# Low parts of every fourth stationary weight piece formed by a negated copy and an accumulating DMA

## Chip, cores and metric

The kernel runs on one core of a Trainium2 chip. The metric is the device time of one execution in microseconds (us). Times of instructions are taken from the hardware profile of one execution.

## What is computed

A trunk of two residual layers on 256 positions of width 2048, all in float32. Layer 0 is sparse attention (an indexer scores all causal keys, each query keeps 64 keys, grouped-query softmax attention follows), layer 1 a gated short convolution; a squared-ReLU MLP of width 8192 stands behind each. Cut to what matters here:

```python
def reference(x, positions, ...):
    for i in range(DEPTH):                       # DEPTH = 2
        j = i // N_MIXERS
        if i % N_MIXERS == 0:
            x = x + _dsa_mixer(_rmsnorm(x, attn_norm_g[j]), attn_w_in[j], ..., attn_w_out[j], positions)
        else:
            x = x + _short_conv_mixer(_rmsnorm(x, conv_norm_g[j]), conv_w_in[j], conv_w[j], conv_w_out[j])
        x = x + _sqrelu_mlp(_rmsnorm(x, mlp_norm_g[i]), mlp_w1[i], mlp_w2[i])
    return x

def _sqrelu_mlp(h, w1, w2):
    a = jax.nn.relu(h @ w1)
    return (a * a) @ w2
```

Nearly all the work is the product of 256 rows with 391 MB of weights, each weight being used once.

## The kernel before

**High and low parts.** A float32 product is made of three products of a shorter format (float32r): each operand is split into a high part (the value rounded) and a low part (the value less its high part), and high x high, high x low and low x high are added in PSUM.

**Pieces.** The weights are cut into 736 pieces, in the order of use. A piece is two k-tiles of 128 rows by 512 columns, laid out as 128 x 1024 elements (in the first two input projections and at the very end one k-tile of 1024 or 1104 columns). Pieces belong to units: one unit accumulates one block of output in PSUM over 4, 8 or 16 pieces, and its end function then takes the banks away. The first 64 pieces (input projection of the attention) and the last 16 have the weights as the moving operand. The 656 between them are "tall": the weights are stationary, and for each 128 x 128 block two matmuls run, line 233 with the high part against 512 columns (high and low parts of the activations) and line 234 with the low part against 256 columns (`matmuls`, lines 219 to 241). A piece is eight such pairs. All tall units begin at a piece number that is a multiple of 4.

**Loads.** One load brings two pieces (1 MB) into one of four `raw` buffers (`load_raw`, lines 178 to 189), issued by SyncE's queue, in order. `split(p)` (lines 196 to 217) makes the two parts of piece p: ScalarE copies the raw piece into `wh`, in float32r (line 211), and VectorE subtracts, `wl` = raw - wh (line 212). Behind the second piece of a load its raw buffer is given up, and the load four ahead of it is issued into the same buffer (line 217).

**Order.** The order on every engine is that in which the program is written: the main loop issues the matmuls of piece p, then the unit's end function if p is its last piece, then one step of every live generator (`step_all`), then the splits up to piece p + 4. `wh` and `wl` have five buffers each, so the split of piece p + 4 can begin when TensorE is through with piece p - 1. Generators are the follow-up work of units that have ended. Of them these matter here: `h_gen` behind each unit of w1 (folds the two halves of each bank on ScalarE and VectorE, lines 825 and 826, squares on VectorE, line 850, then multiplies twice by the row factors on GpSimd, line 856, and `put_pair` writes the `hq` tiles, lines 818 and 819); `y_gen` and `by_gen` of the convolution (GpSimd multiplications in lines 895 and 919); and `rowsT_gen`, which at each norm runs three rounds of a square-root iteration on GpSimd (`newton`, lines 255 to 258, then line 376). Before the change GpSimd issues no DMA.

Of the kernel before, what the change touches and what calls it, by code (L numbers as in the profile page):

```python
# [11 lines left out]
F32 = mybir.dt.float32  # L12
F32R = mybir.dt.float32r
I32 = mybir.dt.int32
AF = mybir.ActivationFunctionType
ALU = mybir.AluOpType
# [57 lines left out]
def trunk(ctx: ExitStack, tc: tile.TileContext, x, positions, attn_norm_g, attn_w_in, attn_q_norm_g,  # L74
          attn_k_norm_g, attn_w_out, conv_norm_g, conv_w_in, conv_w, conv_w_out, mlp_norm_g,
          mlp_w1, mlp_w2, inv, out):
    nc = tc.nc
# [10 lines left out]
    def sbt(shape, tag, bufs, dt=F32):  # L88
        return sb.tile(shape, dt, name=nm(tag), tag=tag, bufs=bufs)

    def shift(n):

        sb.tile([P, n // 4], F32, name=nm("shift"))
# [97 lines left out]
    def load(r):  # L191
        if r < len(raws):
            for _ in load_raw(r):
                pass

    def split(p):
        if p >= len(pieces):
            return
        u, i, r = pieces[p]
        w = u.kk * u.n  # L200
        src = raw_tiles[r][:, (i % 2) * w : (i % 2 + 1) * w]
        if p == 0:
            shift(448)
        hi = sbt([P, WPITCH], "wh", AHEAD + 1, F32R)
        if p == 0:
            shift(64)
        lo = sbt([P, WPITCH], "wl", AHEAD + 1, F32R)
        c = 0
        for v in u.widths if p == 0 else [w]:
            a = slice(c, c + v)  # L210
            nc.scalar.activation(hi[:, a], src[:, a], AF.Copy)  # L211
            nc.vector.tensor_tensor(lo[:, a], src[:, a], hi[:, a].bitcast(F32), ALU.subtract)  # L212
            c += v
        piece_tiles[p] = (hi, lo)
        if p + 1 == len(pieces) or pieces[p + 1][2] != r:
            del raw_tiles[r]
            load(r + RAWS)
# [821 lines left out]
    ps = None  # L1039
    step_all()  # L1040
    split(0)
    split(1)
    live.append(const_gen())
    live.append(rope_tables())
    ahead = 2
    for p in range(len(pieces)):
        matmuls(p)
        u, i, _ = pieces[p]
        if i == u.ticks - 1:
            u.end(u.banks)  # L1050
            u.banks = None
            if u.then is not None:
                live.append(u.then())
        step_all()
        while ahead < p + 1 + (AHEAD if p >= 6 else 2):
            split(ahead)
            ahead += 1
        if p == 15:
            TP = 3
# [22 lines left out]
```

## Time and profile before

| | |
|---|---|
| time, median of 2 runs | 2078.76 us (2078.75 to 2078.77) |
| time of the profiled execution | 2079.38 us |
| its span in the profile | 2077.6 us |
| mean granted clock of TensorE | 1.0 of full speed |
| busy: TensorE / VectorE / ScalarE / GpSimd | 2071.3 / 1446.3 / 1056.9 / 298.8 us |
| loads of weights | 390.94 MB on SyncE's queue |

The span is the time from the first to the last instruction in the profile; the execution's own time is somewhat longer. A busy share is an average over the span. What an engine's idle time is worth depends on whether anything on the chain that ended last waits for that engine. Engines are named as in the profile: PE is TensorE's matmul, PEld its weight load, DVE is VectorE, ACT ScalarE, POOL GpSimd, SP SyncE; an engine's name with a q is its instruction queue. A row of a timeline has the start, the duration, the engine, the line, the operation and its operands, and in brackets how long the engine was idle before it and what released it.

### The profile page before, as it was taken

To read this page: it belongs to the slowest core of one execution; us is meant where nothing else is said; L and a number is where in the kernel's file an instruction comes from. 1 tells how busy PE (TensorE), PEld (TensorE's weight loads), DVE (VectorE), ACT (ScalarE), POOL (GpSimd) and SP (SyncE) were. 2 spreads that over 40 slices of the span, in tenths; PEclk is the share of its full clock that TensorE was granted. 3 is DMA by queue.
4 is the path that set the end of the run, shared out by engine and by line. 5 is a ranking of instruction groups with operands and counts; after the bars stand their busy time and mean duration, and the time that the engine had idled before them with its cause. 6 is when DMAs were issued, how large, how long until landed. Compare 5 with 4: busy or idle time off the path is not lost.

```text
span 2077.6 us, 29879 instructions
## 1 busy us (share of the span) xinstructions
PE 2071.3 (100%) x11880; PEld 1818.1 (88%) x11880; DVE 1446.3 (70%) x1841; ACT 1056.9 (51%) x1549; POOL 298.8 (14%) x294
## 2 busy tenths in 40 slices
PE   9999999999999999999999999999999999999999
PEld 9878888888888888888888888888888888888887
DVE  6487777767667676767866676667676776767755
ACT  7456555544445444544644454555454544545443
POOL 1233105100101001010231110132010010100100
PEclk9999999999999999999999999999999999999999
DMA  8544356566565665665556655565656656665563
GB/s 300 162 142 163 132 177 199 186 200 196 189 203 183 199 191 197 195 193 196 190 182 203 200 185 185 200 188 199 191 193 203 187 196 186 202 199 186 189 193 106
DMA packets 191836, 392.86 MB, mean 189 GB/s; under 512 B 6752, under 2 KB 8016, under 8 KB 191696
## 3 DMA queue, kind: packets, MB, share of 16 engines
q1 hardware_dynamic: 191664, 390.94, 58.6%
q8 instruction: 93, 1.52, 0.3%
q14 instruction: 47, 0.39, 0.1%
q10 hardware_dynamic: 32, 0.01, 0.0%
HBM read 388.83 MB, written 2.10 MB: 188 GB/s over the span
## 4 chain that ended last, share of the span: by engine, by line
PE 99%; DMA 0%; SPq 0%; DVE 0%; issue 0%; DVEq 0%
PE ps L233 57%; PE ps L234 29%; PE ps L240 4%; PE ps L239 4%; PE ps L238 3%; PE ps L723 1%; PE ps L569 0%; PE ps L781 0%; DMA hq<-in_x 0%; PE ps L768 0%; PE ps L431 0%; PE ps L708 0%; SPq L998 0%; PE ps L301 0%; PE ps L364 0%; DVE hq L449 0%
## 5 line engine op out<-in xcount | busy, mean ns | idle before, releaser
L212 DVE TENSOR_TENSOR wl<-raw,wh 128x1024 fp32r<-128x1024 f32 (+2 forms) x738 | 945.6, 1284 | 394.1 <-ACT wh L211 391.0
L211 ACT ACTIVATE wh<-raw 128x1024 fp32r<-128x1024 f32 (+2 forms) x738 | 779.2, 1058 | 517.8 <-PE ps L233 438.0
L233 PE MATMUL ps<-xp,wh 128*128 128x512 f32 x2816 | 960.1, 389 | 0.0
L233 PE MATMUL ps<-hq,wh 128*128 128x512 f32 x2432 | 829.3, 390 | 0.0
L234 PE MATMUL ps<-xp,wl 128*128 128x256 f32 x2816 | 777.3, 276 | 0.0
L234 PE MATMUL ps<-hq,wl 128*128 128x256 f32 x2432 | 671.3, 276 | 0.0
L233 PEld LDWEIGHTS ps<-xp,wh 128*128 128x128 f32 x2816 | 528.6, 188 | 109.4
L233 PEld LDWEIGHTS ps<-hq,wh 128*128 128x128 f32 x2432 | 456.5, 188 | 95.1 <-issue 0.5
L234 PEld LDWEIGHTS ps<-xp,wl 128*128 128x128 f32 x2816 | 528.6, 188 | 0.1
L234 PEld LDWEIGHTS ps<-hq,wl 128*128 128x128 f32 x2432 | 456.5, 188 | 0.5 <-issue 0.5
L825 ACT ACTIVATE half<-ps 128x256 f32<-128x256 f32 x464 | 164.1, 382 | 280.2 <-PE ps L234 280.0
L826 DVE TENSOR_TENSOR tmp<-ps,half 128x256 f32<-128x256 f32 x464 | 183.6, 419 | 172.1 <-ACT half L825 171.9
L856 POOL TENSOR_TENSOR tmp<-tmp,tmp 128x512 f32<-128x512 f32 x64 | 123.8, 1953 | 1086.3 <-DVE tmp L850 594.7
L238 PE MATMUL ps<-wh,xp 128*128 128x512 f32 (+2 forms) x288 | 113.4, 394 | 0.0
L240 PE MATMUL ps<-wl,xp 128*128 128x512 f32 (+2 forms) x288 | 108.0, 375 | 0.3 <-DVE wl L212 0.3
L239 PE MATMUL ps<-wh,xp 128*128 128x512 f32 (+2 forms) x288 | 107.9, 375 | 0.0
L415 DVE TENSOR_TENSOR xT<-xT,tmp 128x512 f32<-128x512 f32 x144 | 99.3, 731 | 0.0
L818 ACT ACTIVATE hq<-tmp 128x512 fp32r<-128x512 f32 x72 | 45.5, 632 | 96.8 <-POOL tmp L856 73.2
L819 DVE TENSOR_TENSOR hq<-tmp,hq 128x512 fp32r<-128x512 f32 x72 | 82.1, 1141 | 5.6 <-ACT hq L818 5.6
L353 POOL TENSOR_TENSOR tmp<-tmp,tmp 128x512 f32<-128x512 f32 x21 | 38.6, 1836 | 254.5 <-ACT tmp L352 185.0
L239 PEld LDWEIGHTS ps<-wh,xp 128*128 128x128 f32 x288 | 54.2, 188 | 10.5 <-issue 2.4
L238 PEld LDWEIGHTS ps<-wh,xp 128*128 128x128 f32 x288 | 54.2, 188 | 10.2 <-issue 2.4
(139 smaller groups left out, 741.1 us busy)
## 6 DMA issues: line engine op xcount, KB each, us to landing
raw<-in_mlp_w SPq DMA_DIRECT2D x256, 1024.0 KB, 5.3
raw<-in_conv_w_in SPq DMA_DIRECT2D x48, 1024.0 KB, 5.2
raw<-in_attn_w_in SPq DMA_DIRECT2D x24, 1024.0 KB, 5.4
raw<-in_attn_w_out SPq DMA_DIRECT2D x16, 1024.0 KB, 5.1
raw<-in_conv_w_out SPq DMA_DIRECT2D x16, 1024.0 KB, 5.1
raw<-in_attn_w_in SPq DMA_DIRECT2D x4, 1104.0 KB, 9.4
raw<-in_attn_w_in SPq DMA_DIRECT2D x7, 552.0 KB, 8.5
out_y<-hq SPq DMA_DIRECT2D x7, 256.0 KB, 2.9
```

Of the source, the lines that this page charges most:

```text
L211: nc.scalar.activation(hi[:, a], src[:, a], AF.Copy)
L212: nc.vector.tensor_tensor(lo[:, a], src[:, a], hi[:, a].bitcast(F32), ALU.subtract)
L233: nc.tensor.matmul(o, wh, xk, start=(k == 0), stop=False)
L234: nc.tensor.matmul(o[:, 0:256], wl, xk[:, 0:256], start=False, stop=(k == K - 1))
L238: nc.tensor.matmul(o[:, :w], ah, wh, start=(k == 0), stop=False)
L239: nc.tensor.matmul(o[:, :w], al, wh, start=False, stop=False)
L240: nc.tensor.matmul(o[:, :w], ah, wl, start=False, stop=(k == K - 1))
L415: nc.vector.tensor_tensor(v, v, r[i], ALU.add)
L819: nc.vector.tensor_tensor(lo, val, hi.bitcast(F32), ALU.subtract)
L825: nc.scalar.activation(h, ps[:, 256:512], AF.Copy)
L826: nc.vector.tensor_tensor(dst, ps[:, 0:256], h, ALU.add)
L856: nc.gpsimd.tensor_tensor(r3, r3, rows_of(key[:-1], "rs2"), ALU.mult)
```

## The change

In tall units, for pieces whose number is 1 mod 4 (the second piece of every second load, 164 pieces), VectorE's subtraction is replaced. ScalarE writes the negated high part into `wl` (line 213 of the new program), and GpSimd issues a DMA that adds the raw piece to it in place (line 214). The other pieces are made as before.

```diff
         for v in u.widths if p == 0 else [w]:
             a = slice(c, c + v)
             nc.scalar.activation(hi[:, a], src[:, a], AF.Copy)
-            nc.vector.tensor_tensor(lo[:, a], src[:, a], hi[:, a].bitcast(F32), ALU.subtract)
+            if u.tall and p % 4 == 1:
+                nc.scalar.activation(lo[:, a], hi[:, a].bitcast(F32), AF.Copy, scale=-1.0)
+                nc.gpsimd.dma_start(lo[:, a], src[:, a], accum_op=ALU.add)
+            else:
+                nc.vector.tensor_tensor(lo[:, a], src[:, a], hi[:, a].bitcast(F32), ALU.subtract)
             c += v
```

Line numbers behind the edit are four higher in the new program: 856 becomes 860, 376 becomes 380, 255 to 258 become 259 to 262.

On GpSimd, at the end of the first MLP's square-root iteration, the program before has this order (the numbers in names are counters of the build):

```order
L258 TENSOR_TENSOR tmp_3404<-tmp_3404,tmp_3402 128x256
L376 TENSOR_TENSOR tmp_3404<-tmp_3404 128x256
L856 TENSOR_TENSOR tmp_3420<-tmp_3420,tmp_3404 128x512
L856 TENSOR_TENSOR tmp_3453<-tmp_3453,tmp_3404 128x512
L856 TENSOR_TENSOR tmp_3613<-tmp_3613,tmp_3404 128x512
L856 TENSOR_TENSOR tmp_3648<-tmp_3648,tmp_3404 128x512
```

At the same place on GpSimd the changed program has the accumulating DMAs among them:

```order
L262 TENSOR_TENSOR tmp_3415<-tmp_3415,tmp_3413 128x256
L380 TENSOR_TENSOR tmp_3415<-tmp_3415 128x256
L214 DMA wl_3494<-raw_3269 128x1024
L214 DMA wl_3579<-raw_3372 128x1024
L860 TENSOR_TENSOR tmp_3431<-tmp_3431,tmp_3415 128x512
L860 TENSOR_TENSOR tmp_3464<-tmp_3464,tmp_3415 128x512
L860 TENSOR_TENSOR tmp_3626<-tmp_3626,tmp_3415 128x512
L860 TENSOR_TENSOR tmp_3661<-tmp_3661,tmp_3415 128x512
L214 DMA wl_3693<-raw_3498 128x1024
L214 DMA wl_3783<-raw_3583 128x1024
```

An accumulate now stands directly behind the iteration, and one directly behind the multiplications of line 860; GpSimd takes its instructions in order.

On SyncE's queue the order is unchanged, and the waits differ. Four loads in the middle of the program, before:

```order
L187 DMA raw_7851<-in_mlp_w 128x4x512 [waits DMAHW2_49,DVE_49]
L187 DMA raw_7908<-in_mlp_w 128x4x512 [waits DMAHW3_49,DVE_49]
L187 DMA raw_7962<-in_mlp_w 128x4x512 [waits DMAHW4_49,DVE_49]
L187 DMA raw_8017<-in_mlp_w 128x4x512 [waits DMAHW5_49,DVE_49]
```

The same four loads on SyncE's queue now (DMASW names a semaphore of GpSimd's DMAs, DMAHW one of SyncE's):

```order
L187 DMA raw_7906<-in_mlp_w 128x4x512 [waits DMAHW2_49,DVE_49]
L187 DMA raw_7964<-in_mlp_w 128x4x512 [waits DMASW7_49,DMAHW3_49,DVE_49,Activation_49]
L187 DMA raw_8018<-in_mlp_w 128x4x512 [waits DMAHW4_49,DVE_49]
L187 DMA raw_8074<-in_mlp_w 128x4x512 [waits DMASW0_49,DMAHW5_49,DVE_49,Activation_49]
```

Every second load now waits for an accumulate too.

## Rows read from the trace of the kernel before

**Rows 1.** The page: busy time, granted clock in 40 slices, chain that ended last.

```profile
PE 2071.3 (100%) x11880; PEld 1818.1 (88%) x11880; DVE 1446.3 (70%) x1841; ACT 1056.9 (51%) x1549; POOL 298.8 (14%) x294
...
PEclk9999999999999999999999999999999999999999
...
PE 99%; DMA 0%; SPq 0%; DVE 0%; issue 0%; DVEq 0%
PE ps L233 57%; PE ps L234 29%; PE ps L240 4%; PE ps L239 4%; PE ps L238 3%; PE ps L723 1%; PE ps L569 0%; PE ps L781 0%; DMA hq<-in_x 0%; PE ps L768 0%; PE ps L431 0%; PE ps L708 0%; SPq L998 0%; PE ps L301 0%; PE ps L364 0%; DVE hq L449 0%
```

**Rows 2.** Groups by form: count | busy us, mean ns | idle before, releasers.

```profile
L212 DVE TENSOR_TENSOR wl<-raw,wh 128x1024 fp32r<-128x1024 f32 x720 | 924.7, 1287 | 385.2 <-ACT wh L211 383.9
...
L211 ACT ACTIVATE wh<-raw 128x1024 fp32r<-128x1024 f32 x720 | 761.2, 1059 | 514.1 <-PE ps L233 438.0 <-PE ps L239 30.4 <-issue 30.0
...
L856 POOL TENSOR_TENSOR tmp<-tmp,tmp 128x512 f32<-128x512 f32 x64 | 123.8, 1953 | 1086.3 <-DVE tmp L850 594.7 <-ACT wh L211 491.5
```

**Rows 3.** Timelines of ACT, POOL and PEld behind one w1 unit.

```profile
893.47 1.06 ACT L211 ACTIVATE wh<-raw 128x1024 fp32r<-128x1024 f32 x1 [1.14 <-PE ps L233]
...
894.64 3.85 POOL L856 TENSOR_TENSOR tmp<-tmp,tmp 128x512 f32<-128x512 f32 x2 [61.44 <-ACT wh L211]
...
903.93 0.19 PEld L234 LDWEIGHTS ps<-xp,wl 128*128 128x128 f32 x1
...
904.27 0.19 PEld L234 LDWEIGHTS ps<-xp,wl 128*128 128x128 f32 x1
```

**Rows 4.** Timelines of ACT and POOL behind the third w1 unit of an MLP.

```profile
371.23 1.06 ACT L211 ACTIVATE wh<-raw 128x1024 fp32r<-128x1024 f32 x1 [0.62 <-PE ps L233]
...
373.00 3.85 POOL L856 TENSOR_TENSOR tmp<-tmp,tmp 128x512 f32<-128x512 f32 x2 [8.69 <-DVE tmp L850]
```

**Rows 5.** Timelines at the ends of three iterations, and line 255's durations (min/median/max).

```profile
349.47 1.06 ACT L211 ACTIVATE wh<-raw 128x1024 fp32r<-128x1024 f32 x1 [1.14 <-PE ps L233]
...
359.22 1.48 POOL L376 TENSOR_TENSOR tmp<-tmp 128x256 f32<-128x256 f32 x1
...
360.27 0.19 PEld L234 LDWEIGHTS ps<-xp,wl 128*128 128x128 f32 x1
...
1055.60 0.61 POOL L376 TENSOR_TENSOR tmp<-tmp 128x256 f32<-128x256 f32 x1
...
1057.47 0.19 PEld L234 LDWEIGHTS ps<-xp,wl 128*128 128x128 f32 x1
...
1405.04 1.62 POOL L376 TENSOR_TENSOR tmp<-tmp 128x256 f32<-128x256 f32 x1
...
1406.51 0.19 PEld L234 LDWEIGHTS ps<-xp,wl 128*128 128x128 f32 x1
...
L255 POOL TENSOR_TENSOR tmp<-tmp x9: 613/1475/1590, 345.4 to 1400.5; 128x256 f32<-128x256 f32 x9
```

**Rows 6.** Timelines of ACT, POOL and PEld in the convolution's input projection.

```profile
1090.27 2.21 POOL L919 TENSOR_TENSOR tmp<-tmp,tmp 128x512 f32<-128x512 f32 x1 [1.83 <-DVE tmp L826]
...
1093.59 1.05 ACT L211 ACTIVATE wh<-raw 128x1024 fp32r<-128x1024 f32 x1
...
1100.99 0.19 PEld L234 LDWEIGHTS ps<-xp,wl 128*128 128x128 f32 x1
```

**Rows 7.** DMA queue (share of 16 engines) and issues: count, KB each, us to landing.

```profile
q1 hardware_dynamic: 191664, 390.94, 58.6%
...
raw<-in_mlp_w SPq DMA_DIRECT2D x256, 1024.0 KB, 5.3
...
raw<-in_attn_w_in SPq DMA_DIRECT2D x4, 1104.0 KB, 9.4
...
out_y<-hq SPq DMA_DIRECT2D x7, 256.0 KB, 2.9
```

**Rows 8.** DMA engines' busy tenths from 895 to 907 us, 40 slices of 0.3 us.

```profile
DMA  9899984100049968799899940018948899899963
```

## Prediction

> **What bounds the kernel now.** I read the page's busy line and the chain of waits first [rows 1]. TensorE is busy 2071.3 of 2077.6 us, and the chain that ended last is TensorE for 99%; VectorE and ScalarE hold 0% of it. So nothing can be won by relieving VectorE: only the 1% ahead of and behind the stream is not TensorE, and the change touches none of it. What can happen is a loss, where TensorE comes to a low part (wl) that is not ready. The question is therefore one of lead: how long before TensorE loads a low part is it finished, and how long will it take in the new way?
>
> Next I read the costliest groups [rows 2] and then the timelines around one piece. A tall piece is eight pairs of matmuls, one pair per 0.34 us (two weight loads of wl stand at 903.93 and 904.27 [rows 3]), so 2.72 us a piece. ScalarE is released by TensorE as soon as a wh buffer is free, and TensorE comes to that piece four pieces later. In rows 3 a piece in the second place of four has its wh copy from 893.47 to 894.53, and its first wl is loaded at 904.27: 9.74 us of lead. That is the usual lead of such a piece.
>
> **The change part by part.** *Removed:* 164 of the 656 tall pieces lose their VectorE subtraction, 164 x 1.287 = 211 us of VectorE [rows 2]. VectorE is not on the chain, so this is worth 0.
>
> *Added on ScalarE:* 164 negations. The trace shows none; the nearest row is the copy of the same shape, 1.06 us [rows 2], so 174 us in all. ScalarE waits some 1.1 to 1.7 us for TensorE ahead of most copies (1.14 us in rows 5), so one 1.06 us more in four pieces lies in that idle time. Price 0, as long as that cover stands.
>
> *Added on the load queue:* every second weight load now waits for the accumulate that still reads its raw buffer, where it waited for a VectorE subtraction. With the accumulate landing some 7 us behind the wh copy, the load starts about 5 us later than now. The load's first piece is split seven pieces later, 19 us behind that copy, and a load lands in 5.3 us [rows 7]: 7 + 5.3 = 12.3 us, so 6 to 7 us of cover is left. Behind it in the queue stands only the next load, which would start about then anyway. Price 0.
>
> *Added as a transfer:* call D the time from "GpSimd free and negation finished" to "TensorE may load wl": issue, transfer, semaphore. The trace has no accumulate and no DMA issued by GpSimd, so D is bounded by rows. Two sizes of plain transfer give a line: 256 KB land in 2.9 us, 1024 KB in 5.3 us [rows 7], so 3.1 us per MB over 2.1 us. A 512 KB piece at a plain copy's price would be 3.7 us: the low end. An accumulate has to read the raw piece and the destination; priced as two passes it is a 1024 KB transfer, 5.3 us. The high end is the 9.4 us of a 1104 KB load at the crowded start [rows 7]. Below 3.7 us I see no reason, and no end below nothing: the transfer adds work and takes none away. I take D = 6.0: the 5.3 us row, and 0.7 us for the share of the 16 DMA engines that weight loads hold meanwhile (58.6% of the span [rows 7], in bursts of 9 tenths and more [rows 8]).
>
> The Trainium skill, "Collectives: The Full Stack", section on why ReduceScatter is half of AllGather, says that an add in the DMA path costs no cycles of its own but needs two source reads, and so runs at half a copy's rate. No trace here shows an accumulate yet; by that rule D is the two-pass estimate, near 5.3 us, and the sum below would be about 15 us.
>
> *The leads, by kind of piece.* (a) An ordinary piece has 9.74 - 1.06 = 8.68 us for D: no stall at 6.0. There are 164 - 36 = 128 of them.
>
> (b) Behind each finished w1 unit GpSimd has two multiplications (64 in the span, 1953 ns each [rows 2]), and the accumulate is queued behind them. In rows 3 they run from 894.64 to 898.49, so D has 904.27 - 898.49 = 5.78 us. At 6.0 this is a stall of 0.22 us. I count 29 such accumulates: 27 like this one, and the one behind the first four multiplications of each MLP, where GpSimd is free at 376.85 and wl is loaded at 371.23 + 10.80 = 382.03 [rows 4], so 5.18 us and a stall of 0.82. Sum 27 x 0.22 + 2 x 0.82 = 7.6 us.
>
> (c) In the convolution's input projection the wh copy itself is late, behind two hq copies: it runs 1093.59 to 1094.64, wl is loaded at 1100.99 [rows 6], so 6.35 - 1.06 = 5.29 us, a stall of 0.71. Four of them: 2.8 us. The second multiplication of this stage (1090.27 now) will queue behind the accumulate's issue, and the next wh copies with it, by 2 to 3 us; they keep some lead.
>
> (d) Three times a square-root iteration of 13 GpSimd instructions stands ahead of an accumulate, and ends near the moment when TensorE wants wl [rows 5]: 360.70 against 360.27, 1056.21 against 1057.47, 1406.66 against 1406.51. Stalls of D + 0.43, D - 1.26 and D + 0.15: 3 D - 0.68 = 17.3 us. The iteration may get shorter by a us, as one subtraction fewer runs beside it (the same instruction takes 613 ns at best and 1475 at the median there); I leave that out.
>
> Sum at D = 6.0: 7.6 + 2.8 + 17.3 = 27.7 us. The profiled execution took 2079.38 us, so 2107.1; the median of the runs shown is 0.6 us below it, so 2106.5 us, +1.3%.
>
> **Rivals.** *The accumulate loses out to the weight loads (slower).* Place: the 29 accumulates behind the multiplications, and (c) and (d) with them. For each us above 5.8 these 36 cost 36 us together, so the time as a function of D is 36 D - 188 us. Two per cent is 41.6 us, which is reached at D = 6.4: that is the point from which it decides. Price at D = 8: 100 us, 2178 us. For it: loads keep the engines 9 tenths busy and more while they run [rows 8], and a delayed load now stands right ahead of the next one, so that two come back to back just ahead of the next accumulate. Against it: loads leave gaps of about as much.
>
> The Trainium skill speaks for this rival: "DMA: Bandwidth & Descriptors", section on issuing engines not being separate DMA queues, says that transfers of all issuing engines run on the same 16 engines and interleave, so that GpSimd's queue gives the accumulate no lane of its own. What the trace shows agrees so far as it goes: loads alone already fill the engines in bursts [rows 8].
>
> *It is late everywhere.* With D above 8.68 all 128 ordinary pieces stall too. At the crowded row's 9.4 us: 128 x 0.72 = 92, and 36 x 9.4 - 188 = 150, together 242 us, 2320 us. For it: an accumulate's rate is unknown, and software issues it. Against it: that row comes from the start, with several loads queued.
>
> *The transfer is hidden.* At D = 3.7 only (d) is left: 3 x 3.7 - 0.68 = 10.4 us, 2089 us; with D below 5 all of (b) and (c) is covered. For it: 512 KB is half a load. Against it: two sources are read.
>
> *Faster.* TensorE would have to be quicker by 41 us with its granted clock at 9 tenths or more in every slice [rows 1] and 6 us of idle time in all. I know of no way.
>
> **How the numbers follow.** Two per cent, 41.6 us, is about what a measurement of this kernel can tell from no change. Forecast (D from 5 to 6.4, up to 41 us): 0.40, with its own range 2092 to 2120. Hidden: 0.18. Loses out to the loads (D 6.4 to 8.7): 0.27. Late everywhere: 0.14. Faster: 0.01. So within 2%: 0.58; slower: 0.41. The range runs from 2084 (hidden, with a shorter iteration) to 2185 (D = 8.2); what it leaves out is nearly all the case that is late everywhere and the upper end of the one before it.
>
> **What would show it.** In the changed kernel's profile VectorE should fall by some 210 us and ScalarE rise by some 174. TensorE should wait for the accumulate at three places for 5 to 6 us each, in 29 places for under 1 us, and nowhere at an ordinary piece. GpSimd's DMAs should land about 6 us behind their issue; beyond 6.4 us the slower rival holds, beyond 8.7 us every fourth piece waits. The forecast is wrong if TensorE waits for wh instead (ScalarE late) or for loads, neither of which is in the sum.

## The result, and the profile after

The changed kernel takes 2156.47 us (median of 2 runs, 2156.18 to 2156.77) against 2078.76 us: ratio 1.0373, interval 1.0356 to 1.039, slower. The forecast was 2106.5 us; the loss is 77.7 us where 27.7 us were predicted. Executions that stand over 1.5% above the fastest of their kernel are left out of the ratios below; this concerns one of eight of e8 and three of ten of e10.

The page after, beside [rows 1, 2, 7]: the span, busy times, DMA engines in 40 slices, DMA queues, the chain that ended last by engine, and groups of instructions.

```profile
span 2155.0 us, 30457 instructions
...
PE 2108.6 (98%) x11880; PEld 1824.7 (85%) x11880; DVE 1205.8 (56%) x1677; ACT 1227.5 (57%) x1713; POOL 395.0 (18%) x458
...
DMA  8444677787887887888888887887788878888873
...
q1 hardware_dynamic: 191664, 390.94, 56.6%
q0 software_dynamic: 23616, 85.99, 20.2%
...
PE 59%; DMA 25%; issue 9%; POOL 3%; ACT 3%; DVE 2%; SPq 0%; POOLq 0%; DVEq 0%; ACTq 0%
...
L238 PEld LDWEIGHTS ps<-xp,wl 128*128 128x128 f32 x2816 | 530.0, 188 | 37.9 <-DMA wl<-raw 37.5
...
L238 PEld LDWEIGHTS ps<-hq,wl 128*128 128x128 f32 x2432 | 456.4, 188 | 32.8 <-DMA wl<-raw 32.2
L214 POOL DMA_DIRECT2D wl<-raw x164 | 141.5, 863 | 1160.8 <-ACT wl L213 1101.3
...
L213 ACT ACTIVATE wl<-wh 128x1024 fp32r<-128x1024 f32 x164 | 174.3, 1063 | 5.2
...
L860 POOL TENSOR_TENSOR tmp<-tmp,tmp 128x512 f32<-128x512 f32 x64 | 94.0, 1496 | 290.9 <-DVE tmp L854 290.9
...
raw<-in_mlp_w SPq DMA_DIRECT2D x256, 1024.0 KB, 6.9
...
wl<-raw POOLq DMA_DIRECT2D x164, 512.0 KB, 9.0
```

The chain was TensorE for 99%; now a quarter of it is DMA, most of that the accumulate. TensorE idles 70.7 us ahead of weight loads of wl (37.9 + 32.8), nearly all of it put down to that DMA. VectorE fell by 240 us and ScalarE rose by 171 us. An accumulate takes 9.0 us from issue to landing where 6.0 us of D were taken, and a weight load 6.9 us where it took 5.3 [rows 7].

The waits of the changed kernel show how this is spread (total us, times, longest):

```profile
PEld ps L238 <- DMA wl<-raw: 69.7, 100, 2.8
```

A hundred waits of 0.7 us on average: not three long ones and a few short ones, but nearly every accumulate in the later part of the program.

**Two regimes.** Rows of the changed kernel's timelines (start, duration, engine), first from 284 to 306 us, then from 693 to 706 us, and last the three stalls behind the square-root iterations:

```profile
290.52 2.45 SPq L187 DMA_DIRECT2D raw<-in_attn_w_out  x2
301.56 2.28 SPq L187 DMA_DIRECT2D raw<-in_mlp_w  x2
...
284.16 1.06 ACT L213 ACTIVATE wl<-wh 128x1024 fp32r<-128x1024 f32 x1
...
285.52 0.85 POOL L214 DMA_DIRECT2D wl<-raw  x1 [10.02 <-ACT wl L213]
296.40 0.86 POOL L214 DMA_DIRECT2D wl<-raw  x1 [10.04 <-ACT wl L213]
...
693.18 0.19 PEld L238 LDWEIGHTS ps<-hq,wl 128*128 128x128 f32 x1 [0.75 <-DMA wl<-raw]
693.27 0.92 SPq L187 DMA_DIRECT2D raw<-in_mlp_w  x2
693.52 1.06 ACT L213 ACTIVATE wl<-wh 128x1024 fp32r<-128x1024 f32 x1
694.88 0.85 POOL L214 DMA_DIRECT2D wl<-raw  x1 [10.85 <-ACT wl L213]
...
704.24 0.19 PEld L238 LDWEIGHTS ps<-xp,wl 128*128 128x128 f32 x1 [0.20 <-DMA wl<-raw]
704.34 0.92 SPq L187 DMA_DIRECT2D raw<-in_mlp_w  x2
705.15 1.06 ACT L213 ACTIVATE wl<-wh 128x1024 fp32r<-128x1024 f32 x1
...
362.94 0.19 PEld L238 LDWEIGHTS ps<-xp,wl 128*128 128x128 f32 x1 [2.84 <-DMA wl<-raw]
...
1088.71 0.19 PEld L238 LDWEIGHTS ps<-xp,wl 128*128 128x128 f32 x1 [2.17 <-DMA wl<-raw]
...
1458.92 0.19 PEld L238 LDWEIGHTS ps<-xp,wl 128*128 128x128 f32 x1 [2.83 <-DMA wl<-raw]
```

The same views' DMA part for the two stretches: the engines' busy tenths in 40 slices, and the issues (count, KB, median us to landing), first 284 to 306, then 692 to 704 us.

```profile
DMA  9999399999000295999999998999960000977999
...
wl<-raw POOLq DMA_DIRECT2D x2, 512.0 KB, 4.9
...
DMA  7300000389747999699999998999999999999986
...
raw<-in_mlp_w SPq DMA_DIRECT2D x2, 1024.0 KB, 8.5
wl<-raw POOLq DMA_DIRECT2D x1, 512.0 KB, 9.3
```

In the early stretch the accumulate is issued at 285.5 us and lands 4.9 us later; the two loads go out at 290.5, behind it. The next round looks the same, and TensorE waits for nothing. In the later stretch two loads go out at 693.3, together, and 1.6 us behind them the accumulate. The engines are full from then on, and it takes 9.3 us. TensorE's waiting load of wl starts at 704.24, and 0.10 us later the next two loads go out, again just ahead of the next accumulate (negation at 705.15).

That is a loop: **the accumulate's landing releases two loads; their 2 MB stand ahead of the next accumulate; it lands late and releases the next two late.** TensorE needs 4 x 2.72 = 10.88 us for four pieces; the loop's rounds begin 11 to 12 us apart (the loads go out at 681.4, 693.3 and 704.3 us), and TensorE waits the difference. From piece 217 on there are 126 accumulates; 107 stall by over 0.1 us, by 0.71 us on average, and from the negation's end to TensorE's use 9.78 us pass on average, where an unstalled piece has 8.64.

**The balance of the trace.** TensorE's weight loads of wl in tall pieces stand 340 ns apart. Everything above that was summed by place from the starts of these loads, for after less before (us):

| | us |
|---|---|
| ahead of ordinary accumulated pieces, class (a) | 49.8 |
| behind GpSimd's multiplications, (b) | 17.1 |
| convolution, (c) | 3.1 |
| behind the square-root iteration, (d) | 8.1 |
| made up again: the second load of such a piece comes 110 ns early | -11.8 |
| pairs at about 350 ns with no wait shown | 7.7 |
| pairs at half the granted clock | 3.2 |
| rest | 0.4 |
| sum (the span grew by 77.4) | 77.6 |

### The profile page after: what moved, and what is told of

It reads as the page before. It is cut to its first block, busy times and chain, and to the rows that moved or that the text cites. A ratio compares the mean times of both kernels' runs of the same rounds, so it can differ in the third digit from the quotient of the medians.

```text
span 2155.0 us, 30457 instructions
## 1 busy us (share of the span) xinstructions
PE 2108.6 (98%) x11880; PEld 1824.7 (85%) x11880; DVE 1205.8 (56%) x1677; ACT 1227.5 (57%) x1713; POOL 395.0 (18%) x458
## 3 DMA queue, kind: packets, MB, share of 16 engines
q0 software_dynamic: 23616, 85.99, 20.2%
## 4 chain that ended last, share of the span: by engine, by line
PE 59%; DMA 25%; issue 9%; POOL 3%; ACT 3%; DVE 2%; SPq 0%; POOLq 0%; DVEq 0%; ACTq 0%
PE ps L237 30%; DMA wl<-raw 19%; PE ps L238 16%; DMA raw<-in_mlp_w 4%; PE ps L243 3%; PE ps L244 3%; PE ps L242 3%; ACT wh L211 2%; DVE wl L216 1%; DMA raw<-in_conv_w_in 1%; POOL tmp L860 1%; ACT wl L213 1%; POOL tmp L262 1%; PE ps L727 0%; POOL tmp L259 0%
## 5 line engine op out<-in xcount | busy, mean ns | idle before, releaser
L216 DVE TENSOR_TENSOR wl<-raw,wh 128x1024 fp32r<-128x1024 f32 (+2 forms) x574 | 705.4, 1232 | 610.1 <-ACT wh L211 608.6
L237 PE MATMUL ps<-xp,wh 128*128 128x512 f32 x2816 | 969.9, 391 | 0.0
L238 PE MATMUL ps<-xp,wl 128*128 128x256 f32 x2816 | 786.5, 279 | 22.3 <-DMA wl<-raw 21.6
L238 PE MATMUL ps<-hq,wl 128*128 128x256 f32 x2432 | 678.4, 279 | 17.7 <-DMA wl<-raw 16.8
L238 PEld LDWEIGHTS ps<-xp,wl 128*128 128x128 f32 x2816 | 530.0, 188 | 37.9 <-DMA wl<-raw 37.5
L238 PEld LDWEIGHTS ps<-hq,wl 128*128 128x128 f32 x2432 | 456.4, 188 | 32.8 <-DMA wl<-raw 32.2
L214 POOL DMA_DIRECT2D wl<-raw x164 | 141.5, 863 | 1160.8 <-ACT wl L213 1101.3
L213 ACT ACTIVATE wl<-wh 128x1024 fp32r<-128x1024 f32 x164 | 174.3, 1063 | 5.2
L860 POOL TENSOR_TENSOR tmp<-tmp,tmp 128x512 f32<-128x512 f32 x64 | 94.0, 1496 | 290.9 <-DVE tmp L854 290.9
L823 DVE TENSOR_TENSOR hq<-tmp,hq 128x512 fp32r<-128x512 f32 x72 | 62.7, 870 | 59.3 <-ACT hq L822 59.3
L243 PEld LDWEIGHTS ps<-wh,xp 128*128 128x128 f32 x288 | 54.1, 188 | 10.4 <-issue 2.4
```

Of the source, the lines that this page charges most:

```text
L213: nc.scalar.activation(lo[:, a], hi[:, a].bitcast(F32), AF.Copy, scale=-1.0)
L214: nc.gpsimd.dma_start(lo[:, a], src[:, a], accum_op=ALU.add)
L237: nc.tensor.matmul(o, wh, xk, start=(k == 0), stop=False)
L238: nc.tensor.matmul(o[:, 0:256], wl, xk[:, 0:256], start=False, stop=(k == K - 1))
L243: nc.tensor.matmul(o[:, :w], al, wh, start=False, stop=False)
L860: nc.gpsimd.tensor_tensor(r3, r3, rows_of(key[:-1], "rs2"), ALU.mult)
```

## The experiments

Theory A is the loop above. Its rivals: B, the accumulates and loads are simply too much for the 16 DMA engines; C, GpSimd's queue (the multiplications ahead of an accumulate) makes them late; D, the stalls behind the square-root iterations set it off. Times are medians; ratios are against the kernel before on the same chip.

**e2: no accumulate.** The low part of those pieces is the negated high part alone.

```diff
-                nc.gpsimd.dma_start(lo[:, a], src[:, a], accum_op=ALU.add)
```

> The accumulating DMA is left out; the low part of these 164 pieces is the negated high part. Only ScalarE's 164 negations and VectorE's relief remain. All theories: 2078 to 2081 us, no wait of TensorE. If ScalarE's added 174 us cost something by themselves, above 2085 us.

2079.02 us, ratio 1.000 (0.9989 to 1.001). ScalarE's 174 us cost nothing; all of the loss comes with the accumulate.

**e4: half as many accumulates.**

```diff
-            if u.tall and p % 4 == 1:
+            if u.tall and p % 8 == 1:
```

> Every eighth piece instead of every fourth (82 accumulates), computing the same. The accumulates behind the square-root iterations are not among them. Theory A: the loop is open, since loads have a second, free pair to spread out before the next accumulate; landing 4.5 to 8 us behind the negation, no stalls, 2078 to 2083 us. Theory B: half the bytes, about half the loss, 2110 to 2125 us. Theory C: half of the accumulates behind multiplications, 2095 to 2120 us.

2079.35 us, ratio 1.000 (0.999 to 1.001). TensorE waits for none of the 82. They are the easy half, though: all 36 places of (b), (c) and (d) have piece numbers of 5 mod 8 and are left out, so this run alone doesn't tell A from B or C. Its issues:

```profile
wl<-raw POOLq DMA_DIRECT2D x82, 512.0 KB, 4.5
```

Spread out like this, an accumulate takes half of the 9.0 us.

**e1: the accumulate reads wh instead of raw**, so that no load waits for it. The low part of those pieces comes out as nothing.

```diff
-                nc.gpsimd.dma_start(lo[:, a], src[:, a], accum_op=ALU.add)
+                nc.gpsimd.dma_start(lo[:, a], hi[:, a].bitcast(F32), accum_op=ALU.add)
```

> The accumulate reads the high part instead of the raw piece, so the low part of these 164 pieces is zero; bytes, issue and order of the accumulates are as in the changed kernel, but a load no longer waits for an accumulate. Theory A (the loop: an accumulate's landing releases two loads at once, and these stand ahead of the next accumulate): accumulates land 4.5 to 6.5 us behind the negation all the way, stalls only at the three square-root iterations, 2082 to 2092 us. Theory B (demand: the engines simply carry too much, whenever loads start): the same bytes, so 2150 to 2160 us. Theory C (GpSimd's queue: accumulates wait behind multiplications): also as the changed kernel, 2150 to 2160 us.

2137.42 us, ratio 1.028 (1.0244 to 1.0317): a miss in size. In the balance the ordinary stalls fall from 49.8 to 7.1 us and those of (b) from 17.1 to 0, as theory A has it. But (d) grew from 8.1 to 18.4 and (c) from 3.1 to 7.6: released by the copy of wh alone, a load now goes out 1.1 us ahead of the negation's end, so an accumulate runs beside one and lands 7.3 us behind its issue (median of the 164). That this is what lengthens the stalls of (c) and (d) is argued. Its waits:

```profile
PEld ps L238 <- DMA wl<-wh: 30.3, 17, 6.3
```

And 15.5 us are pairs at 350 ns, of which more in the last section.

**e5: the load that waits for the accumulate is held back behind the next one**, within the one pool of four raw buffers.

```diff
-            load(r + RAWS)
+            if u.tall and p % 4 == 1:
+                held.append(r + RAWS)
...
+            else:
+                load(r + RAWS)
+                while held:
+                    load(held.pop())
```

> Computes the same, with the same accumulates and waits, but of each two loads the one that waits for no accumulate is issued first, and the one that waits for the accumulate second, so that it holds nobody up. Theory A: the two loads are no longer released by one event; landing 4.5 to 8 us behind the negation, stalls only at the three iterations, 2082 to 2100 us. Theories B and C: 2150 to 2160 us.

2153.61 us, ratio 1.036 (1.0342 to 1.0377). Not the test that was meant. The edit also reserves a buffer for the load held back (a line that is not shown), but it was again the first of the two loads that got the buffer which the accumulate reads, so the wait stood in front as before. The trace agrees: an accumulate lands at 922.97 us, and the two loads go out at 923.11 and 923.57. Two loads that are issued together, in SyncE's order (the lower counter is the load held back):

```text
L190 DMA raw_1784_9810<-in_conv_w_in 128x4x512 [waits DMASW0_49,DMAHW6_49,DVE_49,Activation_49]
L190 DMA raw_1772_9750<-in_conv_w_in 128x4x512 [waits DMAHW5_49,DVE_49]
```

**e7: the same, with the raw buffers in two pools**, so that the load which waits for the accumulate is really the second.

```diff
-        t = raw_tiles[r] = sbt([P, 2 * WMAX], "raw", RAWS)
+        t = raw_tiles[r] = sbt([P, 2 * WMAX], f"raw{r % 2}", RAWS // 2)
```

> The raw buffers are split into two pools of two, one for the loads whose buffer an accumulate reads, one for the others, and of each two loads the one without that wait is issued first; now that one really waits for VectorE alone. Computes the same. Theory A (loop through the two loads that one landing releases): the loop is open, ordinary pieces do not stall; the waits behind the iterations (some 11 us) and in the convolution (3 us) stay, and a slow rhythm of TensorE of 350 ns a pair may cost up to 30: 2090 to 2120 us. Theory B (demand): 2145 to 2160 us.

2128.28 us, ratio 1.0213 (1.0144 to 1.0283). The time is above the range expected, and the four executions lie far apart (2109.95 to 2141.33 us), but the stalls at issue are nearly gone in the profiled one (2137.46 us): (a) 49.8 to 4.6 us, (b) 17.1 to 0. Its issues and waits:

```profile
raw<-in_mlp_w SPq DMA_DIRECT2D x256, 1024.0 KB, 6.0
wl<-raw POOLq DMA_DIRECT2D x164, 512.0 KB, 6.2
...
PEld ps L244 <- DMA wl<-raw: 21.2, 8, 5.7
```

Eight waits are left of a hundred, and the accumulate lands in 6.2 us. The time went elsewhere: 16.8 us at the three iterations and 31.9 us of pairs at 350 ns.

**e10: e7, and the seven accumulates of (c) and (d) back on VectorE.**

```diff
+LATE = (109, 365, 493, 381, 405, 429, 453)
...
-            if u.tall and p % 4 == 1:
+            if u.tall and p % 4 == 1 and p not in LATE:
```

> As e7_swap_two_pools, but the seven pieces that stand behind an iteration (three) or have a late high part in the convolution (four) are made by VectorE again, so 157 accumulates. Computes the same. Theory A with the slow rhythm as a consequence of stalls: hardly a stall is left to start it; 2079 to 2085 us. Theory B (demand): 157 of 164 accumulates remain, 2110 to 2140 us as e7. If the slow rhythm starts without a stall: 2090 to 2130 us.

2079.39 us, ratio 1.0002 (0.9991 to 1.0012). In seven of its ten executions 157 of the 164 accumulates cost next to nothing; the other three took 2114.35 to 2122.80 us, and no trace shows why (see the last section). In the trace the two loads still often go out within 0.5 us of each other (at 913.62 and 914.08, for example), but now 1.3 us behind the accumulate's landing (912.30) and 5 us ahead of the next accumulate (918.96). Its DMA queue and its row of the table by stretches from 700 to 800 us (busy us of PE, PEld, DVE, ACT, POOL; granted clock, share of the DMA engines, GB/s):

```profile
q0 software_dynamic: 22608, 82.32, 20.2%
...
700.00:800.00 100.00, 100.00 (x591) 88.44 (x590) 53.01 (x68) 57.46 (x74) 14.10 (x14) 1.00 0.84 252
```

The changed kernel's rows of the same table:

```profile
700.00:800.00 100.00, 97.10 (x559) 83.98 (x558) 53.32 (x72) 56.84 (x76) 13.42 (x13) 1.00 0.82 228
1480.00:1545.00 65.00, 65.00 (x384) 57.46 (x384) 36.83 (x50) 38.06 (x53) 8.01 (x8) 1.00 0.82 242
```

Theory B falls: e10 moves more (252 GB/s, share 0.84) than the changed kernel does while it stalls (228, 0.82), and the changed kernel runs without a stall from 1480 to 1545 us at the same share.

**e11: the seven back on VectorE, loads in the old order.**

> The changed kernel without its seven late accumulates, loads in the order of the changed kernel. Computes the same. Theory A: the multiplications on GpSimd still push the loop over, some 11 us of waits go and the ordinary pieces keep most of their 50: 2125 to 2150 us. If the stalls behind the iterations are what starts the loop: 2079 to 2095 us.

2142.55 us, ratio 1.0304 (1.0276 to 1.0333). Its waits and issues:

```profile
PEld ps L239 <- DMA wl<-raw: 43.9, 66, 1.5
...
wl<-raw POOLq DMA_DIRECT2D x157, 512.0 KB, 7.6
```

With nothing left at (c) and (d), 34.4 us stand at (a) and 15.3 at (b). So the loop doesn't need the stalls behind the iterations (theory D falls). Between e10 and e11 only the order of the two loads differs, with the two pools that make it hold: 63 us between the medians. In e11's profile 42 us of its loss are stalls at (a) and (b) (less what is made up again) and 27 us are pairs at 350 ns, so not all of the 63 us are the loop's waits.

**e9: the multiplications of line 860 on VectorE**, so that GpSimd's queue is free for the accumulate.

```diff
-            nc.gpsimd.tensor_tensor(r3, r3, rows_of(key[:-1], "rs2"), ALU.mult)
+            nc.vector.tensor_tensor(r3, r3, rows_of(key[:-1], "rs2"), ALU.mult)
```

> The changed kernel with the multiplication by the row factors in each w1 unit on VectorE (which has the time now), so that no accumulate stands behind one on GpSimd. Computes the same. Theory A: the loop may still be pushed over by the iterations; where it is, ordinary pieces stall as before: 2100 to 2155 us. Theory C (GpSimd's queue is the cause): 2085 to 2100 us.

2142.04 us, ratio 1.0302 (1.0255 to 1.0349). Of (b) 3.0 us are left, of (a) still 25.9; about half of the profiled execution's loss, 35 us, are now pairs at 350 ns, which is why the time hardly falls. GpSimd's queue adds to the loop (without it, less than half of its stalls are left), but the loop stands without it: theory C falls as the sole cause.

**e3: a plain copy in place of the accumulate** (`accum_op` left out). The low part of those pieces is the raw piece itself.

> The DMA copies the raw piece over the low part instead of adding to it, so the low part of these 164 pieces is the raw piece; all waits and the order stay. A 4 KB row should take about half of the accumulate's 0.33 us, so 1.3 us less a transfer. Theory A: the loop of landing, two loads and next transfer gets shorter than four pieces of TensorE (11.5 - 1.3 = 10.2 against 10.88 us), so it does not hold TensorE: 2085 to 2105 us. Theory B: half of the added demand goes, 2110 to 2125 us.

2105.56 us, ratio 1.0127 (1.005 to 1.0205), just above theory A's range. Its queue and issues:

```profile
q0 software_dynamic: 23616, 85.99, 11.4%
...
wl<-raw POOLq DMA_DIRECT2D x164, 512.0 KB, 3.2
```

The same bytes in the same packets take 11.4% of 2089.9 us, 238 us of the 16 engines, where the accumulate takes 20.2% of 2155.0, 435 us: 1.83 times. The copy lands in 3.2 us and no loop forms ((a) 0, (d) 2.8 us); the rest of the loss of the profiled execution (2091.64 us) is 10.2 us of pairs at 350 ns. The other execution took 2119.48 us, and no trace shows it.

**e6: five raw buffers instead of four.**

```diff
-RAWS = 4
+RAWS = 5
```

> The changed kernel with five raw buffers instead of four; computes the same. Theory A: a load still starts when an accumulate gives its buffer up, and the next one behind it, so nothing changes: 2145 to 2165 us. Theory D (too few buffers, a deeper prefetch would absorb it): 2090 to 2110 us.

2166.74 us, ratio 1.0422 (1.0355 to 1.0488), just above theory A's range. More room for loads is no cure: TensorE never waited for a load, and the two still go out together. The stalls at (a) and (b) are fewer all the same, 31.3 and 8.4 us in the profiled execution (2154.73 us), and 29 us are pairs at 350 ns.

**e8: one accumulate alone**, at piece 109 behind the first MLP's iteration (`p == 109`).

> One accumulate only, at the piece behind the first MLP's square-root iteration; computes the same. One stall of TensorE of 2 to 4 us, and perhaps 1.5 us of half clock. If TensorE's slow rhythm (350 ns a pair) lasts after a stall until something else resets it, up to 20 us more in all: 2085 to 2105 us. If it does not last: 2081 to 2085 us.

2084.02 us, ratio 1.0023 (1.0013 to 1.0034). Its one wait:

```profile
362.87 0.19 PEld L238 LDWEIGHTS ps<-xp,wl 128*128 128x128 f32 x1 [3.10 <-DMA wl<-raw]
```

3.1 us of the 4.8 lost are this stall; 1.6 us more are pairs at half the clock behind it.

None of these kernels beats the kernel before: e2, e4 and e10 equal it. In e10's profile TensorE is busy for 100% of the span, as before, so there is nothing for VectorE's relief to win.

## Why the prediction was wrong

**What held.** The change cannot win, as TensorE is the chain: e2, e4, e10. VectorE's removed work is worth 0. ScalarE's negations cost 0 (e2), and at 1063 ns one they have the copy's price. The two-pass price of the transfer was about right: alone an accumulate lands 4.5 us behind its issue (e4), against 5.3 estimated. The rule of the Trainium skill, "Collectives: The Full Stack", section on why ReduceScatter is half of AllGather, that the add needs two source reads and so has half a copy's rate, agrees: 1.83 times a copy's engine time (after against e3).

**The step that failed** is the load queue's: "Behind it in the queue stands only the next load, which would start about then anyway. Price 0." I looked at whether the delayed load would be in time for its own piece, and it is. I did not ask what it runs into. Held back until the accumulate lands, it goes out together with the next load, just ahead of the next accumulate, on the same 16 engines. e10 against e11 puts this step's price at 63 us, with the pairs at 350 ns that come with it; in the changed kernel the stalls at (a) and (b) are 66.9 us of the loss.

**The step that followed from it** is the constant D = 6.0 for all classes. D depends on what stands ahead of the accumulate, and that feeds itself from round to round. Up to piece 213 (640 us) an accumulate lands 4.5 to 7.6 us behind its issue, within its lead; from 217 on, with a pair of loads just ahead, mostly 8 to 10 us (median 9.2). At piece 213 the accumulate is issued late, behind a pair of multiplications, and lands 8.6 us behind its negation, at the very end of its lead; 217 comes at 8.9 us, and from there the loop holds up to the third iteration (piece 493), is off behind it, and sets in again at 529. Each landing is told by sixteen updates of a semaphore: at 213 fifteen had come by 645.09 us and the last came at 647.29, the widest such gap of the run, and ahead of it a packet of 16 KB of the queue that the page calls "instruction" ran from 645.21 to 646.15. That this packet tipped the loop over is argued from the times alone; ahead of 529 no update is that late, and the landings creep from 6.4 us behind the negation at 513 to 9.0 at 529. So "(a) no stall" became 49.8 us, and (b) 17.1 where 7.6 were priced.

I wrote the mechanism down, in the rival that "loses out to the weight loads" ("two come back to back just ahead of the next accumulate"), but charged it to the 36 places with small leads only. Whoever shares the engines with the loads shares them at all 164. The Trainium skill, "DMA: Bandwidth & Descriptors", section on issuing engines not being separate DMA queues, has the transfers of all issuing engines share the same 16 engines. The trace agrees: an accumulate alone took 4.5 us, behind two loads 9.3, and its first packet came 4.7 us behind its issue there (piece 233) where it came 1.4 us behind it at piece 85. "Late everywhere" had the right places and too high a price, the whole of D - 8.68 for each. But a stall delays TensorE and not the next piece's copy, which TensorE has released before it stalled, so each stall lengthens the next lead. In the rows above D is 704.24 - 694.58 = 9.66 us; the lead 8.64, plus the 0.75 of the stall before, leaves 0.27, and 0.20 is the wait in the row. In a steady loop a stall is half of D - 8.64: (9.78 - 8.64) / 2 = 0.57, and 0.60 was measured on average over the 126. 110 ns of each are made up at the next pair besides.

The measured time lies inside the stated range, and "loses out to the weight loads" gives it at D = 7.4 (36 x 7.4 - 188 = 78 us). That is luck: 49.8 us of it stand at ordinary pieces, which that rival had at nothing.

**The small terms.** (c) was priced at 2.8 us and is 3.1, by luck: D is 7.2 to 7.6 us there instead of 6.0, and the lead had grown from 5.29 to between 6.5 and 6.9. (d) was priced at 17.3 and is 8.1, for two reasons. D is 4.5 us there: line 380 ends at 358.42, and wl is loaded at 362.94. And the iteration ends earlier: 358.42 where it was 360.70 [rows 5], so "I leave that out" left out 2.3 us of the first stall. The cause is the piece's own subtraction: in e8, where only that one is gone, the iteration ends at 358.20; in e10, where it is back, at 360.16.

## What to carry to other kernels

When a DMA becomes the reader of a buffer that loads are waiting for, follow its landing to the loads that it releases, and those loads to the next DMA of its kind: if they meet on the same engines, a latency that fits its lead alone can lock into a loop. Price a transfer at two values, alone and behind what its own completion releases, and compare the second with the lead. What opened the loop here is order, not room: let the load that waits for the slow reader be the last in the queue (e7, e10). More buffers (e6) and fewer instructions on the issuing engine (e9) left 39.7 and 28.9 of the 66.9 us of stalls, and the time where it was.

## What the runs showed of the hardware that was not expected

**A slower rhythm of TensorE without a wait.** In many of the kernels TensorE's pairs run at some 350 ns instead of 340 for hundreds of microseconds, at full granted clock. e7 from 700 to 800 us, by stretch and by group (count, busy us, mean ns):

```profile
700.00:800.00 100.00, 100.00 (x573) 87.62 (x573) 53.99 (x73) 57.44 (x77) 13.41 (x13) 1.00 0.79 233
...
L243 PE MATMUL ps<-xp,wh 128*128 128x512 f32 x148 | 51.9, 395 | 0.0
...
L244 PE MATMUL ps<-xp,wl 128*128 128x256 f32 x147 | 41.2, 280 | 0.0
```

573 matmuls pass where the kernel before has 590 in the same stretch, the 512-column one at 395 ns and not 389, with no idle time. 3232 pairs of e7 run so, 32.3 us; 805 pairs after. In the profiles it often begins behind a stall of TensorE and ends at another one, but in e7 one stretch began at 650.1 us with no stall in the trace, and e6 ran so from its first tall pieces on. What triggers it stays open. In e5, e6, e9 and e11 it is 27 to 36 us of the loss. It is not in the traces of the kernel before, e2, e4, e8 and e10. But three executions of e10 and one of e8 took 35 to 49 us longer than the others of their kernel, about 10 ns for each of several thousand pairs, where none of 45 executions of the kernel before took over 2080.2 us; that the rhythm is the reason is argued, as no trace shows these executions.

**A subtraction on VectorE doubles a GpSimd instruction that runs beside it.** That GpSimd is slower at times could be read from [rows 5], but I gave it no weight. Lines of the iteration in e8 show both sizes, and VectorE's subtraction beside the longer one:

```profile
354.60 0.74 POOL L260 TENSOR_TENSOR tmp<-tmp 128x256 f32<-128x256 f32 x1
...
355.92 1.59 POOL L262 TENSOR_TENSOR tmp<-tmp,tmp 128x256 f32<-128x256 f32 x1
...
355.43 1.47 DVE L216 TENSOR_TENSOR wl<-raw,wh 128x1024 fp32r<-128x1024 f32 x1 [1.39 <-ACT wh L211]
```

The multiplications of line 860 follow the same pattern: 1953 ns before [rows 2], 1935 in e4 and 1944 in e8, where VectorE still subtracts the pieces beside them, and 1496 in the changed kernel and 1512 in e2, where it doesn't.

**Half the clock behind some stalls.** The changed kernel behind the third iteration, by stretch:

```profile
1459.00:1464.00 5.00, 5.00 (x20) 4.34 (x21) 0.07 (x1) 1.16 (x2) 2.95 (x3) 0.66 0.84 177
```

TensorE had waited 2.83 us up to 1458.92. Its first pairs then ran at 340 ns, and from 1460 us on pairs took 640 ns for 3.4 us: the lower of its two levels, 1.2 GHz instead of 2.4. The stall of 2.84 us at 362.94 was followed by the same, and each of the two costs some 1.6 us more than itself. The length of a stall alone doesn't tell which ones: the stall of 2.17 us at 1088.71 was followed by no such pairs, but neither was one of 2.83 us in e9 (at 1457.28 us; the granted clock from 1457 to 1462 us was 1.00) nor one of 3.16 us in e1 (at 1262.28 us). In e1, behind its three waits of some 6 us, half the clock lasts 6.8 us each time. What decides it stays open.
